# A branch moved between two k-tiles, a split subtraction across it, a weight load on ScalarE's queue and a small chain on GpSimd, in a hybrid decoder layer

## The chip, the core and the metric

One core of a Trainium2 chip runs the whole layer in one launch. The metric is the device time in microseconds (us), the median over runs. The kernel before takes 609.99 us (three runs, 609.93 to 610.08).

## The reference

The inputs are a residual stream x of 512 tokens by 1024, an embedding p of 512 by 256, and the layer's weights, all float32. Cut to what matters here:

```
x = x + hybrid_mixer(rms_norm(x)) @ ...            # GLA heads, gated conv, W_out
h = rms_norm(x); group_logits = h @ w_group + b_group; exp_logits = h @ w_router + b_router
# top 1 of 4 groups, top 2 of the 4 experts in it; weights = p_grp * softmax top 2, renormed
for e in range(16): y += combine[:, e] * ((silu(h @ w_gate[e]) * (h @ w_up[e])) @ w_down[e])
x = x + y
x = x + sigmoid(rms_norm(x) @ w_ple_gate) * (p @ w_ple_proj)   # the embedding product is p @ w_ple_proj
out = rms_norm(x)
```

## The kernel before, in words

Every float32 product is made of three matmuls: operand and weight are each split into a high part (a rounded copy, made by ScalarE) and a low part (value minus high part, a subtraction on VectorE), and TensorE multiplies high by high, high by low and low by high. `Stream` (lines 51 to 150) brings the weights in: `load` (83) takes a free slot and issues a DMA of 1 MB, by default on SyncE's queue (SP); `split` (103) makes the high part at once and returns the low part as a function if `later=True`; the low part of a slot's second half gives the slot back (`give`, 73), and that issues the next load.

The order of work on every engine is the order of the source; nothing is rearranged. Around the change it is this. The mixer's output product ends, its tokens are routed (`route`, `rank`), and meanwhile TensorE computes the embedding product p @ w_ple_proj in sixteen steps `ple(0)` to `ple(15)` (line 810). An output block of 128 x 512 takes two of them, one for each k-tile, of three matmuls each; after the second ScalarE copies the block out of PSUM. The steps fill TensorE's time while VectorE does the routing.

`lo0`, `lo1` and `lo2` (1037, 1048, 1067) are the low parts of the first three half slots of expert 0's gate weights; `lo0` has run early, `lo1` belongs to a second half, so that it gives its slot back, and `lo2` to a first half. `fullest` (948) finds how many tokens the fullest expert has. An expert has 96 places; `overflow` (1174) reads the number into a register on every engine and branches (1177): if an expert has more tokens than that, a handler computes the rest. With these inputs it does not run. The handler calls `weights`, `norms` and `weights2` itself and, in loops, loads 24 pieces of weights by SP (8 for gate, 8 for up, twice 4 for down).

After the branch come the routing weights: `weights` (956; two exponentials on ScalarE among it), `norms` (975; the tokens' RMS factors cut into three bfloat16 parts and put into `vals`, columns 5 to 7), `weights2` (986; columns 2 to 4 of `vals`), a one-hot for expert 2, `lo1`, the last embedding steps, the transposes of expert 0's gathered rows, the matmuls `slots(..., 2, 8)` that read `vals`, `lo2`, and then expert 0's gate product (`pg0`) and 16 experts with it. Two gathers on GpSimd's queue, issued just ahead of the branch, fetch the rows of experts 0 and 1. `W.free.append((ring, "x1")); W.load()` (1269) puts a freed buffer of x to use as a slot, and loads the next weights into it.

Two things of the built program are not seen in the source. Transfers issued by SP and by ScalarE count their completion on eight semaphores in turn, and each transfer waits, on the queue that issues it, until the transfer eight before it has landed. And where a branch is not taken, every engine waits on the way out until its own instructions ahead of the branch are done, and then adds to its semaphores what the handler would have added; SP does this for the eight transfer semaphores, one after the other in a fixed order, and so waits there for every transfer issued ahead of the branch.

Of the kernel before, what the change touches and what calls it, by code (L numbers as in the profile page):

```python
# [14 lines left out]
OP = mybir.AluOpType  # L15
# [3 lines left out]
P = 128  # L19
S = 512  # L20
D = 1024
NT = S // P
# [6 lines left out]
NE = 16  # L29
# [122 lines left out]
def hymba_layer(ctx, tc, x, p, g_mix, w_in, w_gla_gate, b_gla_gate, g_gla_out, w_conv, w_out,  # L152
# [4 lines left out]
    p, w_in, w_out = p[0, 0], w_in[0], w_out[0]  # L157
    ve, se, pe, ge, sy = nc.vector, nc.scalar, nc.tensor, nc.gpsimd, nc.sync
# [15 lines left out]
    def mm_ps(name):  # L174
        return ps.tile([P, HALF], F32, tag="mm", name=name)
# [4 lines left out]
    def half(i):  # L180
        return slice(i * HALF, (i + 1) * HALF)

    def tok(t):
        return slice(t * P, (t + 1) * P)


    W = Stream(nc, hlp, 6)
# [22 lines left out]
    Aa, Af = (consts.tile([P, NT, NG, EPG], BF16, name=f"A{i}") for i in range(2))  # L210
    key = consts.tile([P, NT, NE], F32, name="key")
    iota1 = consts.tile([P, CAP], BF16, name="iota1")
    vals = consts.tile([P, NT, NE, 8], BF16, name="vals")
# [596 lines left out]
    def ple(j):  # L810

        i, k = divmod(j, 2)
        t, ci = divmod(i, 2)
        if j < 2:
            wp.extend(W.take())
        if k == 0:
            pps_[i] = mm_ps(f"pp{t}_{ci}")
        (xh, xl), (wh, wl) = pT[k], wp[k]
        for n, (a, b_) in enumerate(((xh, wh), (xh, wl), (xl, wh))):
            pe.matmul(pps_[i], a[:, tok(t)], b_[:, half(ci)], start=(k + n == 0), stop=(k == 1 and n == 2))  # L820
        if k:
            ple_out(i)
        if j == 15:
            W.done(2)

    def ple_out(i):
        t, ci = divmod(i, 2)
        prj_[t, ci] = prjs[t // 2][1][:, half(2 * (t % 2) + ci)]
        se.copy(prj_[t, ci], pps_[i])
# [100 lines left out]
    def slots(e, oh, vals, toki, rowi, sw, name, c0=0, c1=8, fill=False):  # L930


        pi = aux_ps(f"pslot{name}_{c0}")
        for t in range(NT):
            pe.matmul(pi[:CAP, c0:c1], oh[:, t, :], vals[:, t, e, c0:c1], start=(t == 0), stop=(t == NT - 1))  # L935
        if c0 == 0:
            sv = small.tile([CAP, 1], F32, tag="sv", name="sv" + name)
            ve.tensor_reduce(sv, pi[:CAP, 0:2], axis=AX.X, op=OP.add)
            if fill:
                ve.tensor_scalar(toki[:, e:e + 1], sv, OUT_OF_RANGE, S - 1.0, op0=OP.add, op1=OP.min)  # L940
            ve.tensor_scalar(rowi[:, e:e + 1], sv, OUT_OF_RANGE, None, op0=OP.add)
        if c1 == 8:
            ve.tensor_reduce(sw[:, e], pi[:CAP, 2:8].rearrange("p (w j) -> p w j", j=3), axis=AX.X, op=OP.add)
# [4 lines left out]
    def fullest():  # L948
        cmax = rtp.tile([P, 1], F32, name="cmax", bufs=1)
        ve.tensor_reduce(cmax, pcnt[:, :NE], axis=AX.X, op=OP.max)  # L950
        ve.tensor_copy(cmaxi, cmax)

    wt = []
    sec = rtp.tile([P, NT, NE], BF16, name="sec", bufs=1)
# [19 lines left out]

    def norms():

        r3 = rtp.tile([P, NT, 3], BF16, name="r3", bufs=1)
        left = rtp.tile([P, NT], F32, name="left", bufs=1)
        for j in range(3):
            src = left if j else rsm  # L980
            ve.tensor_copy(r3[:, :, j], src)
            if j < 2:
                ve.tensor_tensor(left, src, r3[:, :, j], op=OP.subtract)
        ve.tensor_copy(vals[:, :, :, 5:8], r3[:, :, None, :].to_broadcast([P, NT, NE, 3]))

    def weights2():
        d_, m, c_, s_ = wt
        z_ = rtp.tile([P, NT], F32, name="z_", bufs=1)
        ve.tensor_reduce(z_, d_, axis=AX.X, op=OP.add)
        ve.scalar_tensor_tensor(z_, m[1], 1.0, z_, op0=OP.add, op1=OP.mult)  # L990
        ve.reciprocal(cw[0], z_)
        ve.tensor_mul(cw[1], cw[0], m[1])

        for d2, a_, c2 in ((c_, Af.rearrange("p t g e -> p t (g e)"), cw[0]), (s_, sec, cw[1])):
            ve.tensor_tensor(d2, a_, c2[:, :, None].to_broadcast([P, NT, NE]), op=OP.mult)
        ve.tensor_tensor(c_, c_, s_, op=OP.add)
        for j in range(2, 5):
            ve.tensor_copy(vals[:, :, :, j], c_)
            if j < 4:
                ve.tensor_tensor(c_, c_, vals[:, :, :, j], op=OP.subtract)  # L1000
# [34 lines left out]
    t = NT - 1  # L1035
# [12 lines left out]
    lo1 = W.split(later=True)  # L1048
# [8 lines left out]
    ple(6)  # L1057
    for e in range(2):
        slots(e, oh01[e], vals, toki, rowi, sw, f"{e}", 0, 2, fill=True)
    ve.tensor_tensor(sec, Aa.rearrange("p t g e -> p t (g e)"), Af.rearrange("p t g e -> p t (g e)"),  # L1060
                     op=OP.subtract)

    pcnt = mm_ps("pcnt")
    for t in range(NT):
        pe.matmul(pcnt[:, :NE], onesb, Aa.rearrange("p t g e -> p t (g e)")[:, t], start=(t == 0), stop=(t == NT - 1))
    fullest()
    lo2 = W.split(later=True)
    mx.close()

# [104 lines left out]
    def overflow(free_x):  # L1174

        many = nc.values_load(cmaxi[0:1, 0:1], min_val=0, max_val=S)
        with tc.If(many > CAP, preferred_fallthrough_block=True, label="crowded"):
            weights()
            norms()
            weights2()  # L1180
            with tc.For_i(0, NE, 1) as ei:
                ke = rt.tile([P, NT], F32, name="ke")
                ve.tensor_copy(ke, key[:, :, bass.ds(ei, 1)].rearrange("p t o -> p (t o)"))
                va_ = rt.tile([P, NT, 8], BF16, name="va_")
                ve.tensor_copy(va_, vals[:, :, bass.ds(ei, 1), :].rearrange("p t o c -> p t (o c)"))

                def product(dst, xT, w, c0, wks):
                    rows_ = w[0, bass.ds(ei, 1)].rearrange("o r c -> (o r) c")
                    for k in range(xT.shape[-1] // CAP):
                        wk = wks[k % len(wks)]  # L1190
                        sy.dma_start(wk, rows_[k * P:(k + 1) * P, c0:c0 + HALF])
                        pe.matmul(dst, xT[:, k * CAP:(k + 1) * CAP], wk, start=(k == 0),
                                  stop=(k == xT.shape[-1] // CAP - 1))

                def turned(dst, src):
                    pt = aux_ps("pt_v")
                    for k in range(4):
                        pe.transpose(pt[:, k * CAP:(k + 1) * CAP], src[:, tok(k)], ident[:CAP, :CAP])
                    ve.tensor_copy(dst, pt[:, :4 * CAP])

                xr, xv, hv, yv = xe[free_x], ye[0][:, :8 * CAP], ye[0][:, :4 * CAP], ye[1][:CAP]
                sv, wa, wb = xr[:CAP, :HALF], xr[:, HALF:], ye[0][:, HALF:]
                with tc.For_i(1, -(-S // CAP), 1):
                    ve.tensor_scalar(ke, ke, float(-CAP), None, op0=OP.add)
                    rw = rt.tile([CAP, 1], I32, name="rw")
                    wv = rt.tile([CAP, 1, 2], F32, name="wv")
                    slots(0, one_hot(0, ke[:, :, None], "v"), va_[:, :, None, :], rw, rw, wv, "v")
                    ge.memset(xr, 0.0)
                    gather(xr[:CAP], rw)
                    for i in range(2):  # L1210
                        turned(xv[:, 4 * CAP * i:4 * CAP * (i + 1)], xr[:CAP, half(i)])
                    pgv, puv = mm_ps("pgv"), mm_ps("puv")
                    product(pgv[:CAP], xv, w_exp_gate, 0, [wa])
                    product(puv[:CAP], xv, w_exp_up, 0, [wa])
                    se.activation(sv, pgv[:CAP], AF.Silu, scale=wv[:, 0, 1:2])
                    ve.scalar_tensor_tensor(sv, puv[:CAP], wv[:, 0, 1:2], sv, op0=OP.mult, op1=OP.mult)
                    turned(hv, sv)
                    for ci in range(2):
                        pdv = mm_ps("pdv")
                        product(pdv[:CAP], hv, w_exp_down, HALF * ci, [wa, wb])  # L1220
                        ve.tensor_scalar(yv[:, half(ci)], pdv[:CAP], wv[:, 0, 0:1], None, op0=OP.mult)
                    scatter(yv, rw)
# [42 lines left out]
    ylast = []  # L1265

    ple(7)
    overflow(0)
    W.free.append((ring, "x1"))
    W.load()  # L1270
    for j in range(8, 11):
        ple(j)
    weights()
    se.preload_act_table_set("silu_and_others")
    norms()
    weights2()
    oh = {2: one_hot(2, key, "2", ve)}
    lo1()
    for j in range(11, 16):
        ple(j)  # L1280
    xTs[0] = transposed(x0[:, half(0)], "xT0a") + transposed(x0[:, half(1)], "xT0b")
    for e in range(2):
        slots(e, oh01[e], vals, toki, rowi, sw, f"{e}", 2, 8)
    lo2()
    W.give((ring, "x0"))
    W.give(pTt[0][0])
    pgs[0] = mm_ps("pg0")
# [34 lines left out]
    e = NE - 1  # L1322
# [181 lines left out]
    t = NT - 1  # L1504
# [63 lines left out]
```

## Time and profile before

| | us |
|---|---|
| median of three runs | 609.99 |
| the profiled execution | 609.77 |
| its span, first to last instruction | 608.1 |

The profiled execution's own time is 1.67 us more than its span, for what lies around it, and 0.22 us under the median. All times of rows are counted from the span's start. In a timeline a row gives start, length, engine, line, operation, what is written and read, and in brackets the idle time ahead of it and what ended it; names with a q (SPq, ACTq) are an engine's queue, which waits, branches and issues DMAs.

### The profile page before, as it was taken

Reading aid. Unit: us, or ns where it says so; the run is one execution under the profiler, and the core shown is the slowest. Engines: PE = TensorE matmul, PEld = TensorE weight load, DVE = VectorE, ACT = ScalarE, POOL = GpSimd, SP = SyncE. Lnnn points to the kernel's source line nnn. Section 1 sums busy time; section 2 is a strip of 40 time slices with the busy share of each in tenths; the row PEclk is TensorE's granted clock in tenths of the full one; section 3 lists DMA queues with packets and bytes.
Section 4 is the critical chain, followed back from the end, with each engine's and each line's share of the span. In section 5 each row is a group of like instructions: output and inputs, shape, how many; then the busy total and the mean of one; then the engine's idle time right before and its main releaser. Section 6 shows DMA issues by size and latency. Waiting matters only on the chain.

```text
span 608.1 us, 8441 instructions
## 1 busy us (share of the span) xinstructions
PE 588.4 (97%) x3026; PEld 450.6 (74%) x3026; DVE 480.1 (79%) x802; ACT 365.0 (60%) x520; POOL 112.6 (19%) x147
## 2 busy tenths in 40 slices
PE   7999999999999999899999999999999999989995
PEld 6997888887687788677777777777777777666884
DVE  4742799874396476799999999999999998879764
ACT  5532537303715333768877888887787897776222
POOL 1440664100420000123210111111011100000111
PEclk9999999999999999999999999999999999999998
DMA  8622221221125948599999999999999989992001
GB/s 282 214 105 71 70 70 69 70 73 68 45 93 210 394 179 306 199 376 361 382 373 364 359 360 345 378 371 360 353 346 357 375 321 373 367 349 85 36 34 70
DMA packets 65292, 146.15 MB, mean 240 GB/s; under 512 B 5205, under 2 KB 5804, under 8 KB 65246
## 3 DMA queue, kind: packets, MB, share of 16 engines
q1 hardware_dynamic: 61342, 136.16, 61.0%
q0 software_dynamic: 3744, 9.15, 6.3%
q8 instruction: 24, 0.39, 0.2%
q10 hardware_dynamic: 160, 0.27, 0.1%
q14 instruction: 22, 0.18, 0.1%
HBM read 137.03 MB, written 12.19 MB: 245 GB/s over the span
## 4 chain that ended last, share of the span: by engine, by line
PE 53%; DVE 4%; issue 1%; ACT 1%; POOLq 0%; DVEq 0%; ACTq 0%
PE pd L1120 15%; PE pg L1120 14%; PE pu L1120 13%; PE pgate L1120 6%; PE pt_xT L1108 2%; PE pgate_last L1521 1%; DVE lo L113 1%; PE pt_hT L1108 1%; DVE lo L118 1%; PE px L1427 1%; ACT hi L112 1%; PE pz L1255 0%; PE pu15b L1344 0%; PE pslot L935 0%; ACT ye L1314 0%
## 5 line engine op out<-in xcount | busy, mean ns | idle before, releaser
L113 DVE TENSOR_TENSOR lo<-raw,hi 128x1024 fp32r<-128x1024 f32 x172 | 203.4, 1218 | 14.1 <-ACT hi L112 14.0
L112 ACT CAST hi<-raw 128x1024 fp32r<-128x1024 f32 x172 | 170.6, 1052 | 0.1
L118 DVE SCALAR_TENSOR_TENSOR lo<-raw,cst,hi 128x512 fp32r<-128x512 f32 (+1 forms) x56 | 44.8, 843 | 16.2 <-ACT hi L117 16.0
L1090 POOL DMA_INDIRECT xe<-xgd,rowi x12 | 19.4, 1614 | 165.0 <-PE pt_xT L1108 158.7
L113 DVE TENSOR_TENSOR lo<-x,hi 128x1024 fp32r<-128x1024 f32 x30 | 36.0, 1219 | 1.7 <-ACT hi L112 1.7
L117 ACT ACTIVATE hi<-raw,cst 128x512 fp32r<-128x512 f32 (+1 forms) x56 | 36.6, 717 | 0.0
L1141 POOL DMA_INDIRECT xd<-ye,rowi x15 | 22.5, 1501 | 49.0 <-ACT ye L1314 45.4
L112 ACT CAST hi<-x 128x1024 fp32r<-128x1024 f32 x30 | 30.8, 1053 | 0.0
L1120 PE MATMUL pg<-hi,xT_1h 128*96 128x512 f32 x60 | 24.4, 407 | 0.0
L1120 PE MATMUL pg<-hi,xT_0h 128*96 128x512 f32 x60 | 23.7, 396 | 0.0
L1120 PE MATMUL pg<-lo,xT_1h 128*96 128x512 f32 x60 | 23.6, 394 | 0.0
L1120 PE MATMUL pg<-hi,xT_1l 128*96 128x512 f32 x60 | 23.6, 393 | 0.0
L1120 PE MATMUL pg<-lo,xT_0h 128*96 128x512 f32 x60 | 23.5, 392 | 0.0
L1120 PE MATMUL pg<-hi,xT_0l 128*96 128x512 f32 x60 | 23.5, 391 | 0.0
L1120 PE MATMUL pu<-hi,xT_0h 128*96 128x512 f32 x56 | 22.9, 409 | 0.0
L1120 PE MATMUL pu<-lo,xT_0h 128*96 128x512 f32 x56 | 22.1, 395 | 0.0
L1120 PE MATMUL pu<-lo,xT_1h 128*96 128x512 f32 x56 | 22.1, 394 | 0.0
L1120 PE MATMUL pu<-hi,xT_1h 128*96 128x512 f32 x56 | 22.1, 394 | 0.0
L1120 PE MATMUL pu<-hi,xT_1l 128*96 128x512 f32 x56 | 22.0, 392 | 0.0
L1120 PE MATMUL pu<-hi,xT_0l 128*96 128x512 f32 x56 | 21.9, 392 | 0.0
L645 ACT ACTIVATE sq<-xs 128x512 f32<-128x512 f32 x4 | 2.5, 631 | 28.5 <-DVE xs L627 28.5
L737 POOL TENSOR_TENSOR xs<-xs,sg 128x128 f32<-128x128 f32 x16 | 11.3, 736 | 44.2 <-ACT sg L732 44.2
(583 smaller groups left out, 1593.7 us busy)
## 6 DMA issues: line engine op xcount, KB each, us to landing
raw<-in_w_exp_gate_dram SPq DMA_DIRECT2D x28, 1024.0 KB, 16.9
raw<-in_w_exp_down_dram SPq DMA_DIRECT2D x27, 1024.0 KB, 13.8
raw<-in_w_exp_up_dram SPq DMA_DIRECT2D x26, 1024.0 KB, 17.8
raw<-in_w_in_dram SPq DMA_DIRECT2D x10, 1024.0 KB, 4.9
x<-in_w_exp_up_dram SPq DMA_DIRECT2D x6, 1024.0 KB, 14.4
x<-in_w_exp_down_dram SPq DMA_DIRECT2D x5, 1024.0 KB, 16.2
xs<-in_x_dram SPq DMA_DIRECT2D x16, 256.0 KB, 5.5
raw<-in_w_out_dram SPq DMA_DIRECT2D x4, 1024.0 KB
```

The costliest lines, as they stand in the source:

```text
L112: self.nc.scalar.copy(hi, rw)
L113: los.append(lambda: eng.tensor_sub(lo, rw, hi.bitcast(F32)))
L117: self.nc.scalar.activation(hi[:, c_], rw[:, c_], AF.Copy, scale=g_)
L118: los.append(lambda c_=c_, g_=g_: eng.scalar_tensor_tensor(lo[:, c_], rw[:, c_], g_, hi[:, c_].bitcast(F32), op0=OP.mult, op1=OP.subtract))
L645: se.activation(osq[c], to[c], AF.Square)
L737: ge.tensor_tensor(tv, tv, sgs[i][:, tok(t)], op=OP.mult)
L1090: ge.indirect_dma_start(out=x_, out_offset=None, in_=xgd, in_offset=bass.IndirectOffsetOnAxis(ap=idx, axis=0), bounds_check=S - 1, oob_is_ ...
L1108: pe.transpose(pt[:, k * n:(k + 1) * n], src[:n, tok(k)], ident[:n, :n])
L1120: pe.matmul(dst, a, b_, start=(k + n == 0), stop=(k == nk - 1 and n == 2))
L1141: ge.indirect_dma_start(out=xd, out_offset=bass.IndirectOffsetOnAxis(ap=idx, axis=0), in_=y_, in_offset=None, bounds_check=S - 1, oob_is_e ...
L1427: pe.transpose(pt[:, tok(k)], X(t)[:, ci * HALF + k * P:ci * HALF + (k + 1) * P], ident)
L1521: pe.matmul(pgl[i][:, :256], a, b_[:, 256 * i:256 * i + 256], start=(k + n == 0), stop=(k == NK - 1 and n == 2))
```

## The change

The branch moves from between `ple(7)` and `ple(8)` to between `ple(8)` and `ple(9)`, the two k-tiles of one block; `lo1` moves ahead of it, `lo2` behind `weights`; `norms` moves to GpSimd and ahead of `weights`; the load into x1's buffer is issued by ScalarE; the subtraction `sec` goes behind `fullest`; in the handler one PSUM block serves both halves of the down product.

```
 def norms():
-            ve.tensor_copy(r3[:, :, j], src)
+            ge.tensor_copy(r3[:, :, j], src)
             if j < 2:
-                ve.tensor_tensor(left, src, r3[:, :, j], op=OP.subtract)
-        ve.tensor_copy(vals[:, :, :, 5:8], ...)
+                ge.tensor_tensor(left, src, r3[:, :, j], op=OP.subtract)
+        ge.tensor_copy(vals[:, :, :, 5:8], ...)
...
-    ve.tensor_tensor(sec, ...)
     pcnt = ...
     fullest()
+    ve.tensor_tensor(sec, ...)
     lo2 = W.split(later=True)
...
+                    pdv = mm_ps("pdv")
                     for ci in range(2):
-                        pdv = mm_ps("pdv")
...
     ple(7)
+    ple(8)
+    lo1()
     overflow(0)
+    ple(9)
     W.free.append((ring, "x1"))
-    W.load()
-    for j in range(8, 11):
-        ple(j)
+    W.load(eng=se)
+    ple(10)
+    norms()
     weights()
     se.preload_act_table_set("silu_and_others")
-    norms()
+    lo2()
     weights2()
     oh = {2: one_hot(2, key, "2", ve)}
-    lo1()
     for j in range(11, 16):
         ple(j)
     ...
-    lo2()
```

## Rows read from the trace of the kernel before

**Rows 1.** The page's busy time of each engine, with its share of the span and its instructions.

```profile
PE 588.4 (97%) x3026; PEld 450.6 (74%) x3026; DVE 480.1 (79%) x802; ACT 365.0 (60%) x520; POOL 112.6 (19%) x147
```

**Rows 2.** The chain of work that ended last, in order of time: start, length, what. The up products of experts 1 and 2 begin here (the second row is cut off by the stretch that was asked for).

```profile
280.53 5.56 PE pu L1120 x24
...
298.41 1.62 PE pu L1120 x7
```

**Rows 3.** Timeline of TensorE: the first embedding matmul behind the branch, the first transpose of expert 0's rows, the slot matmuls, the first and the third matmul of expert 0's gate product.

```profile
248.36 0.47 PE L820 MATMUL pp<-hi,raw 128*128 128x512 f32 x1 [1.49 <-DVEq L1177]
...
254.05 0.49 PE L1108 MATMUL pt_xT0a<-ident,xe 96*128 96x96 f32 x4
...
254.71 0.48 PE L935 MATMUL pslot<-vals,oh 128*96 128x6 bf16 x8
255.26 0.47 PE L1120 MATMUL pg<-hi,xT0ah 128*96 128x512 f32 x1
...
256.24 0.47 PE L1120 MATMUL pg<-hi,xT0al 128*96 128x512 f32 x1 [0.27 <-DVE xT0al L1100]
```

**Rows 4.** The queues at the branch (lines 1176 and 1177): operation, count, shortest, median and longest in ns, first and last start in us.

```profile
L1176 ACTq TENSOR_LOAD <-cmaxi x1: 473/473/473, 246.9 to 246.9; - x1
...
L1177 SPq EVENT_SEMAPHORE  x8: 6/17/703, 248.3 to 249.8; - x8
...
L1177 PEldq COMPARE_BRANCH  x1: 397/397/397, 247.6 to 247.6; - x1
...
L1177 DVEq EVENT_SEMAPHORE  x1: 21/21/21, 248.2 to 248.2; - x1
```

**Rows 5.** Timeline of VectorE ahead of the branch (sec, cmaxi) and behind it: the start of `norms`, the start of `weights2` and its second operation, its last, `lo1`.

```profile
246.47 0.18 DVE L1060 TENSOR_TENSOR sec<-A,A 128x64 bf16<-128x64 bf16 x1
...
246.76 0.15 DVE L951 CAST cmaxi<-cmax 128x1 int32<-128x1 f32 x1
...
249.86 0.17 DVE L981 CAST r<-rsm 128x4 bf16<-128x4 f32 x1
...
251.04 0.16 DVE L989 TENSOR_REDUCE z__2535<-d__2513 128x4 f32<-128x16 f32 x1
251.32 0.16 DVE L990 SCALAR_TENSOR_TENSOR z__2535<-m,z__2535 128x4 f32<-128x4 f32 x1
...
253.77 0.31 DVE L998 CAST vals<-c__2518 128x64 bf16<-128x64 f32 x1
...
254.50 1.22 DVE L113 TENSOR_TENSOR lo<-raw,hi 128x1024 fp32r<-128x1024 f32 x1
```

**Rows 6.** Timeline of ScalarE around the branch: the copy of `ple(7)`'s block, the table load behind the branch, the copy of `ple(9)`'s block, the two exponentials, the next table load.

```profile
246.91 0.58 ACT L829 COPY raw<-pp 128x512 f32<-128x512 f32 x1 [0.57 <-PE pp L820]
247.81 1.28 ACT L829 ACT_TABLE_LOAD   x1 [0.33 <-ACTq L1177]
250.03 0.59 ACT L829 COPY raw<-pp 128x512 f32<-128x512 f32 x1 [0.93 <-PE pp L820]
250.51 0.22 ACT L963 ACTIVATE d__2513<-d__2513 128x16 f32<-128x16 f32 x1
250.63 0.19 ACT L973 ACTIVATE m<-m 128x4 f32<-128x4 f32 x1
250.84 1.28 ACT L1274 ACT_TABLE_LOAD   x1
```

**Rows 7.** SP's queue behind the branch: timeline rows of the load into x1's buffer and of the load into `lo1`'s slot, and, from line 98's own view, the wait ahead of the second (started at 250.4).

```profile
249.95 0.41 SPq L98 DMA_DIRECT2D x<-in_w_exp_up_dram  x1
255.78 0.38 SPq L98 DMA_DIRECT2D raw<-in_w_exp_up_dram  x1
...
L98 SPq EVENT_SEMAPHORE  x1: 5342/5342/5342, 250.4 to 250.4; - x1
```

**Rows 8.** DMA. First what the queue of SP's loads moved in the first and the last of the four microseconds (252 to 253, 255 to 256) in which the load into x1's buffer moved: packets, MB, share of the 16 engines; all four together 500 packets and 1.01 MB. Then the page's issues of two loads of the same size: count, KB each, median us from issue to landing.

```profile
q1 hardware_dynamic: 43, 0.09, 50.6%
...
q1 hardware_dynamic: 124, 0.23, 59.0%
...
raw<-in_w_in_dram SPq DMA_DIRECT2D x10, 1024.0 KB, 4.9
...
raw<-in_w_ple_proj_dram SPq DMA_DIRECT2D x1, 1024.0 KB, 7.9
```

**Rows 9.** A DMA issued by ScalarE's queue (the last output): shortest, median, longest in ns.

```profile
L1540 ACTq DMA_DIRECT2D out_dram<-ye x1: 409/409/409, 604.0 to 604.0; - x1
```

**Rows 10.** The two gathers. GpSimd's timeline row of the second; then, from the view of their tile, us from issue to landing of the first (issued 247.13) and of the second.

```profile
248.57 0.98 POOL L1090 DMA_INDIRECT xe<-xgd,toki  x1 [0.30 <-DVE gm L960]
...
DMA to landing us min/median/max: 4.7/4.7/4.7
...
DMA to landing us min/median/max: 6.5/6.5/6.5
```

**Rows 11.** Elementwise work on GpSimd elsewhere: a one-input operation on 20 columns and a two-input one on 128 columns, shortest, median and longest in ns.

```profile
L323 POOL TENSOR_SCALAR wr<-wr,cst x8: 328/329/385, 30.1 to 32.3; 128x20 f32<-128x20 f32 x8
...
L737 POOL TENSOR_TENSOR xs<-xs,sg x16: 458/904/914, 160.0 to 170.5; 128x128 f32<-128x128 f32 x16
```

**Rows 12.** The end of the span: TensorE's last matmul in its timeline, and one row of the stretches of 1 us, where after the busy times of PE, PEld, DVE, ACT and POOL comes the granted clock of TensorE (1.00 is 2.4 GHz), then the DMA share and GB/s. The rows of the stretches ahead of it have 1.00, those behind it 0.50.

```profile
600.20 0.27 PE L1521 MATMUL pgate_last<-raw,x2l 128*128 128x256 f32 x1
...
603.00:604.00 1.00, 0.00 (x0) 0.00 (x0) 0.72 (x2) 0.72 (x1) 0.25 (x1) 0.55 0.00 0
```

More of the change, by code (lines that the diff above doesn't have):

```diff
@@ L980, in norms @@
             src = left if j else rsm
-            ve.tensor_copy(r3[:, :, j], src)
+            ge.tensor_copy(r3[:, :, j], src)
             if j < 2:
-                ve.tensor_tensor(left, src, r3[:, :, j], op=OP.subtract)
-        ve.tensor_copy(vals[:, :, :, 5:8], r3[:, :, None, :].to_broadcast([P, NT, NE, 3]))
+                ge.tensor_tensor(left, src, r3[:, :, j], op=OP.subtract)
+        ge.tensor_copy(vals[:, :, :, 5:8], r3[:, :, None, :].to_broadcast([P, NT, NE, 3]))
     def weights2():
@@ L1059, in hymba_layer @@
         slots(e, oh01[e], vals, toki, rowi, sw, f"{e}", 0, 2, fill=True)
-    ve.tensor_tensor(sec, Aa.rearrange("p t g e -> p t (g e)"), Af.rearrange("p t g e -> p t (g e)"),
-                     op=OP.subtract)
     pcnt = mm_ps("pcnt")
@@ L1066, in hymba_layer @@
     fullest()
+    ve.tensor_tensor(sec, Aa.rearrange("p t g e -> p t (g e)"), Af.rearrange("p t g e -> p t (g e)"),
+                     op=OP.subtract)
     lo2 = W.split(later=True)
```

## The prediction

> **What bounds the kernel.** I read the page first: TensorE is busy for 97% of the span [rows 1]. Then the chain in order of time: from expert 1 to expert 2 it is TensorE alone, 17.88 us for one expert (298.41 - 280.53), and between 285 and 500 us the waits name none of TensorE's [rows 2]. So what is gained or lost ahead of expert 0 moves everything behind it by as much. Then the timelines between 246 and 256 us, where TensorE does wait: 1.49 us at the branch and 0.27 us ahead of the third matmul of expert 0's gate product [rows 3]. That third matmul, at 256.24, is my mark: the work behind it is the same in both kernels, and I take its shift as the change of the time.
>
> **The parts that help.** `ple(8)` moves into the branch's idle time: three matmuls. Behind the branch TensorE now does 24 in 5.69 us (254.05 - 248.36) [rows 3], 0.237 each, so it saves 0.71 us and reaches the transposes at about 253.35. The branch path itself is some 1.3 us long: the register load starts at 246.9, and VectorE's last wait of it ends at 248.2 [rows 4]. `lo1`, 1.22 us, goes behind `cmaxi` and `sec` on VectorE. It would start at about 246.9 (where `cmaxi` ends now; `sec` behind it gives back at most its own 0.18) and end at 248.1 [rows 5], ahead of VectorE's release at 248.2. That a queue loads its register while its engine works is seen on ScalarE, where both start at 246.9 [rows 4, 6]; if VectorE did not, the branch would come up to 1.2 us later there. Behind the branch VectorE loses `lo1` (1.22) and `norms` (249.86 to 251.04, 1.18) and gets `lo2` (the same shape as `lo1`, 1.22) [rows 5], so it is free for the low part of expert 0's rows 1.18 us sooner.
>
> `norms` on GpSimd: six small operations. No row has these shapes there. The nearest from below is 0.33 us for one input and 20 columns, from above 0.91 us for two inputs and 128 columns [rows 11]; six are 2.0 to 5.5 us, and since the columns are few I take 2.0 and keep 5.5. GpSimd is free when the second gather's issue ends, 249.55 [rows 10], so `vals` has its last columns at 251.5 to 255.0. `weights2` writes the others until 254.08 now [rows 5]. At the lower price this costs nothing, at the upper it is a rival below. The handler's PSUM block costs nothing, since the handler does not run.
>
> **The part that hurts.** `lo1` gives its slot back, and that issues a load of 1 MB on SP: today at 255.78, 0.06 us after `lo1` ends (254.50 + 1.22 = 255.72), SP having stood at that wait for 5.34 us [rows 5, 7]. With `lo1` ahead of the branch, SP issues it at about 248.15, ahead of the branch too. On the way out of the branch SP walks over eight transfer semaphores: that is the x8 row, seven of them over in nanoseconds today since nothing is in flight on them, and the longest 0.70 us [rows 4]. Now one of them belongs to the load just issued, and SP stands there until it has landed.
>
> SP itself could afford that: its next loads were due behind the transposes. But the load into x1's buffer, which the change gives to ScalarE, takes the next semaphore in turn: the load of `lo1`'s slot is the last transfer ahead of the branch, the handler's 24 are three full turns, and x1's is the first behind. Before a transfer is issued its queue waits for that semaphore with the handler's count added, and SP adds this only after it has passed the semaphore ahead of it, the one it stands at. I read this order in the instructions of the program before (there x1's load waits for its semaphore with the handler's count, and SP walks in ascending order), not in a view; the view shows the eight waits, and x1's load directly behind them at 249.95 [rows 4, 7]. So ScalarE, which works in order, stands at its DMA until the other load has landed. Behind it in its queue are the two exponentials, the table load and three copies; VectorE's `weights2` waits for the exponentials, the slot matmuls for `weights2`, and in TensorE's order expert 0's gate product stands behind them.
>
> The Trainium skill says in DMA: Bandwidth & Descriptors, section Anatomy of one DMA, that DMA engines wait on no semaphore and that every such wait is made by the issuing queue ahead of the DMA; the 5.34 us wait on SP's queue agrees [rows 7]. Its section Issuing engines are not separate DMA queues says that a second issuing engine saves only the time of issuing: by that rule the move to ScalarE could be worth at most one issue, 0.41 us [rows 7].
>
> Now the sum for ScalarE's stand. Issue at 248.15. For the landing the nearest row is x1's load today: the same size, the same gathers in flight; issued at 249.95, its last bytes come in the microsecond to 256, so about 5.85 us [rows 7, 8]. The bounds are 4.9 and 7.9 us, other 1 MB loads [rows 8]. I take 5.85: landed at 254.0. Then 0.05 for the semaphores (a guess from rows of 17 ns [rows 4]), ScalarE's issue 0.41 [rows 9]: 254.46. Exponentials 250.51 to 250.82, 0.31 [rows 6]: 254.8. From VectorE's use of the second one to the end of `weights2`, 254.08 - 251.32 = 2.76 [rows 5]: 257.6. Slot matmuls, 255.26 - 254.71 = 0.55 [rows 3]: 258.15. The first two matmuls of the gate product at 0.32 each, as at 248.36 and its successor, 0.64: the third at 258.8. The rows' high part is ready by then on ScalarE (254.8 + table 1.28 + three copies of 0.59 = 257.85, plus 0.5 for the part itself, 258.35) [rows 6], and VectorE's low part shortly behind, inside the same 0.64. So 258.8 - 256.24 = **2.6 us later**; with the bounds, 1.6 and 4.6. The loads lose nothing by it: one is 7.6 us earlier, and x1's at 254.1 still stands ahead of where the second load is now.
>
> The profiled execution took 609.77, 0.22 under the median, so 609.99 + 2.6 = 612.6 is the forecast, and by itself its range is 611.4 to 614.7.
>
> **The rivals.** *The clock falls in the gap.* TensorE would do next to nothing from 254.0 to 257.6, 3.6 us. At the end of the span its last matmul ends at 600.47, and the granted clock falls from 2.4 to 1.2 GHz inside 603 to 604, 2.5 to 3.5 us after it [rows 12]. So the fall can happen here. A matmul of 0.237 would cost as much again; for how many no row shows, and I price it at a stretch as long as the gap itself: 3.6 us at half speed lose 1.8 us, 614.4. The Trainium skill, TensorE: Matmul & The Clock Gate, section What's actually happening, says that the throttled clock is the default and activity releases it; the fall in the tail agrees, and nothing here shows the release. Against it: the gap is little longer than the idle time ahead of that fall.
>
> *Nobody stands.* If x1's load draws a semaphore that SP has passed, or the landing is not waited for, ScalarE issues it at about 249.9 and has the exponentials done by 250.8, as now [rows 6]. `lo2` covers them, `weights2` ends at about 254.0, and TensorE, at the transposes 0.7 us earlier, starts the gate product at about 254.5 and its third matmul, with the low part in time, at 255.15: 1.1 us gained, 608.9, bounds 0.7 and 1.4 (TensorE no longer waits for VectorE's release). That is the other side. For it speaks that the load leaves SP's queue at all; against it the walk over eight semaphores [rows 4]. The price at which it turns is plain: ScalarE's stand costs nothing while the landing comes before 251.4 (254.0 - 2.6), 3.3 us after the issue, and no 1 MB row is under 4.9 [rows 8]. The first gather shares the engines with the earlier load then; its 4.7 us may become the second's 6.5 [rows 10], 253.6 against 253.35, 0.3 us at most.
>
> *GpSimd is the bound.* If nobody stands and `norms` costs 5.5 us, `vals` is full at 255.0, the slots end at 255.6 and the third matmul comes at 256.25: no change, 610.0. If ScalarE stands, 255.0 is before 257.6 and GpSimd is hidden.
>
> **How the numbers follow.** ScalarE stands, clock up: 0.60. It stands and the clock falls: 0.13. Nobody stands: 0.20. GpSimd bounds or the gain is eaten elsewhere: 0.07. A measurement of this kernel can tell about 0.2%, 1.2 us, from no change. The first two are slower by more: 0.73. Of the third, centred on 1.1 us, a little under half is faster by more than 1.2, so 0.09; the rest and the fourth are the same, 0.18. The predicted time is the first case's, 612.6. To hold 8 in 10 the range reaches from the faster case, 608.8, to the first case's upper bound, 614.7, which takes in the fallen clock as well.
>
> **What would show it.** In the changed profile: SP's load of `lo1`'s slot at about 248.2, ahead of SP's walk, and one long wait of 5 to 6 us in that walk; a wait of some 4 us on ScalarE's queue ahead of its DMA, that ends right after SP's; the exponentials at about 254.5, `weights2` ending near 257.6, TensorE idle between the transposes and the slots; `norms` on GpSimd over by 252; `lo1` inside the branch. It is wrong if ScalarE's DMA goes out near 250 and TensorE's third matmul comes before 256.2; then nobody stood. If the walk has its long wait but ScalarE does not, it was the order of the semaphores that I misread. A granted clock under 1.00 behind the gap is the first rival.

## The result, and the profile after

| | us |
|---|---|
| before, median (lowest to highest) | 609.98 (609.93 to 610.08) |
| after, median (lowest to highest) | 616.88 (615.67 to 617.63) |
| ratio, with its 95% interval | 1.0106 [1.0094, 1.0118] |
| the profiled execution of after, and its span | 617.63, 615.9 |

The change costs 6.9 us, 1.1%; the forecast was 612.6. Numbers of lines are one higher than before (1121 for 1120, 1178 for 1177).

**TensorE** first: its timeline, as in [rows 3].

```profile
253.09 0.39 PE L820 MATMUL pp<-hi,raw 128*128 128x512 f32 x1
257.19 0.87 PE L1109 MATMUL pt_xT0a<-ident,xe 96*128 96x96 f32 x4 [3.71 <-DMA xe<-xgd,toki]
...
260.27 0.80 PE L935 MATMUL pslot<-vals,oh 128*96 128x6 bf16 x8 [1.57 <-DVE vals L999]
260.93 0.72 PE L1121 MATMUL pg<-hi,xT0ah 128*96 128x512 f32 x1
...
261.88 0.63 PE L1121 MATMUL pg<-hi,xT0al 128*96 128x512 f32 x1
```

The chain in order of time, expert 1's up product, which answers to the first of [rows 2]:

```profile
288.40 5.56 PE pu L1121 x24
```

TensorE waits twice: 3.71 us for the first gather, ahead of the transposes, then 1.57 us for `vals`, ahead of the slots. The second wait ends last: the gather has landed and is transposed by then. The third matmul of expert 0's gate product, the mark, comes at 261.88, 5.64 us later than in [rows 3]. Expert 1's up product starts 288.40 - 280.53 = 7.87 us later [rows 2], as much as the two executions' own times differ (617.63 - 609.77 = 7.86). So 2.23 us more are lost behind the mark, with no wait named: that is the clock. The stretches of 1 us, columns as in [rows 12], show its fall and its return:

```profile
255.00:256.00 1.00, 0.00 (x0) 0.00 (x0) 0.00 (x0) 0.00 (x0) 0.00 (x0) 1.00 0.80 180
256.00:257.00 1.00, 0.00 (x0) 0.00 (x0) 0.00 (x0) 0.04 (x1) 0.00 (x0) 0.82 0.15 49
257.00:258.00 1.00, 0.81 (x5) 0.84 (x6) 0.62 (x5) 0.98 (x3) 0.00 (x0) 0.50 1.03 45
...
266.00:267.00 1.00, 1.00 (x4) 0.60 (x3) 0.51 (x1) 0.00 (x0) 0.00 (x0) 0.56 1.03 401
267.00:268.00 1.00, 1.00 (x6) 0.73 (x5) 0.00 (x0) 0.00 (x0) 0.00 (x0) 1.00 1.07 424
```

TensorE has been idle since 253.48 (253.09 + 0.39); inside 256 to 257 the granted clock leaves 2.4 GHz for 1.2, and only inside 266 to 267 does it come back. Between, a matmul of the gate product starts every 0.43 us (261.45 to 261.88), where 0.23 is usual.

**SP and ScalarE**, the queues of [rows 4, 6, 7]. First SP's timeline, the load into `lo1`'s slot; then the walk, in the view of its line (columns as in [rows 4]):

```profile
248.41 0.38 SPq L98 DMA_DIRECT2D raw<-in_w_exp_up_dram  x1
```

```profile
L1178 SPq EVENT_SEMAPHORE  x8: 17/17/17, 250.2 to 256.6; - x8
```

And ScalarE's timeline from the copy behind the branch:

```profile
249.42 0.59 ACT L829 COPY raw<-pp 128x512 f32<-128x512 f32 x1
256.49 0.42 ACTq L98 DMA_DIRECT2D x<-in_w_exp_up_dram  x1
256.96 0.22 ACT L963 ACTIVATE d__2523<-d__2523 128x16 f32<-128x16 f32 x1 [6.95 <-SPq L1178]
257.08 0.19 ACT L973 ACTIVATE m<-m 128x4 f32<-128x4 f32 x1
```

The load goes out ahead of the walk; the walk, 1.5 us long before, lasts from 250.2 to 256.6. ScalarE stands behind it: its DMA goes out at 256.49, and the exponentials, at 250.51 before, run at 256.96, after 6.95 us of idle time whose releaser is SP's walk.

**VectorE and GpSimd**, answering to [rows 5, 10, 11]. VectorE's timeline: `lo1`, the first operation behind the branch, the start of `weights2` and its last.

```profile
247.16 1.22 DVE L113 TENSOR_TENSOR lo<-raw,hi 128x1024 fp32r<-128x1024 f32 x1
248.53 0.17 DVE L960 TENSOR_REDUCE gm<-lg 128x4 f32<-128x16 f32 x1
...
257.21 0.17 DVE L990 TENSOR_REDUCE z__2538<-d__2523 128x4 f32<-128x16 f32 x1 [5.84 <-ACT d__2523 L963]
259.91 0.31 DVE L999 CAST vals<-c__2528 128x64 bf16<-128x64 f32 x1
```

GpSimd's timeline: the two gathers, the first and the last operation of `norms`.

```profile
247.46 1.92 POOL L1091 DMA_INDIRECT xe<-xgd,toki  x1 [5.53 <-DVE sec L1066]
249.68 0.98 POOL L1091 DMA_INDIRECT xe<-xgd,toki  x1 [0.30 <-DVE s__2529 L970]
250.67 0.74 POOL L982 CAST r<-rsm 128x4 bf16<-128x4 f32 x1
...
252.57 0.47 POOL L985 COPY vals<-r 128x192 bf16<-128x192 bf16 x1
```

And the first gather's tile: us from issue to landing, 4.7 before.

```profile
DMA to landing us min/median/max: 9.6/9.6/9.6
```

`lo1` lies inside the branch, as forecast. `norms` is over at 253.04, inside the 251.5 to 255.0 of the forecast's sum, though not by 252 as its signs had it. The first gather is not as forecast: issued at 247.46, it lands at about 257.1. What moved in its place stands in the DMA queues (columns as in [rows 8]; q1 carries SP's loads, q0 the gathers), for the microseconds from 250, 251, 252 and 253:

```profile
q1 hardware_dynamic: 134, 0.27, 75.3%
...
q1 hardware_dynamic: 184, 0.38, 98.7%
...
q1 hardware_dynamic: 148, 0.28, 81.7%
q0 software_dynamic: 22, 0.09, 22.0%
...
q0 software_dynamic: 68, 0.25, 90.7%
q1 hardware_dynamic: 28, 0.05, 18.7%
```

In the kernel before, q0 moved 75 packets in 250 to 251; here it moves none until 252.5, when 442 of the load's 528 packets are through, and has most of its packets after 253.

So there are three suspects: ScalarE's stand behind SP's walk, the gather behind the early load, and the clock. The first two run side by side, so one profile can't price them: here the chain that ends last goes through ScalarE's DMA, the exponentials and `vals`, and the gather is hidden behind it, but it might take the chain's place if the stand were gone. My theory is the forecast's, that the stand carries the loss; its rivals are that the gather does, and that the clock does.

### The profile page after: what moved, and what is told of

Read it like the earlier page. It is cut to its first block, busy times and chain, and to the rows that moved or that the text cites. A ratio compares the mean times of both kernels' runs of the same rounds, so it can differ in the third digit from the quotient of the medians.

```text
span 615.9 us, 8438 instructions
## 1 busy us (share of the span) xinstructions
PE 592.7 (96%) x3026; PEld 453.7 (74%) x3026; DVE 479.1 (78%) x796; ACT 365.0 (59%) x520; POOL 115.6 (19%) x153
## 4 chain that ended last, share of the span: by engine, by line
PE 52%; DVE 3%; ACT 1%; issue 1%; POOLq 0%; ACTq 0%; DVEq 0%
PE pg L1121 15%; PE pd L1121 14%; PE pu L1121 13%; PE pgate L1121 5%; PE pt_xT L1109 2%; PE pgate_last L1524 1%; DVE lo L113 1%; PE pt_hT L1109 1%; DVE lo L118 1%; ACT hi L112 1%; PE px L1430 1%; PE pz L1256 0%; PE pslot L935 0%; ACT L1394 0%; ACT ye L1317 0%
## 5 line engine op out<-in xcount | busy, mean ns | idle before, releaser
L118 DVE SCALAR_TENSOR_TENSOR lo<-raw,cst,hi 128x512 fp32r<-128x512 f32 (+1 forms) x52 | 42.1, 849 | 16.2 <-ACT hi L117 16.0
L117 ACT ACTIVATE hi<-raw,cst 128x512 fp32r<-128x512 f32 (+1 forms) x52 | 34.1, 718 | 0.0
L1317 ACT ACTIVATE ye<-pd,sw 96x512 f32<-96x512 f32 x30 | 19.0, 683 | 1.0 <-PE pd L1121 1.0
```

The lines of the kernel that those rows point to most:

```text
L117: self.nc.scalar.activation(hi[:, c_], rw[:, c_], AF.Copy, scale=g_)
L118: los.append(lambda c_=c_, g_=g_: eng.scalar_tensor_tensor(lo[:, c_], rw[:, c_], g_, hi[:, c_].bitcast(F32), op0=OP.mult, op1=OP.subtract))
L1317: se.activation(y_[:, half(ci)], pds[ci][:CAP], AF.Copy, scale=sw[:, e, 0:1])
```

## The experiments

Diffs are against the changed kernel, if nothing else is said. Each time is set against runs of the kernel before on the same chip (medians 610.09 to 610.14); the kernel after itself, run again on one of these chips, took 615.78 (615.54 to 615.91).

**1. The load back on SP.** Takes away ScalarE's stand alone.

```
-    W.load(eng=se)
+    W.load()
```

> The changed kernel, but x1's load is issued by SP again. Theory S (the time is ScalarE's stand at its DMA behind SP's walk): the exponentials run near 250, the slots near 254.5, and the time falls to about 609, under the kernel before. Theory G (the load of lo1's slot, issued just ahead of the branch, also starves the first gather, and TensorE waits for that by itself): the exponentials run near 250 as well, but the transposes still wait for the gather until about 257 and the granted clock still falls; the third matmul of the gate product comes at about 260 instead of 261.9, so some 614.5 to 615.5.

Measured: 614.09 (613.01 to 615.43), ratio 1.0067 [1.0047, 1.0087]. The exponentials run at 249.68. TensorE's timeline at the transposes, and the clock in two stretches:

```profile
256.19 0.87 PE L1109 MATMUL pt_xT0a<-ident,xe 96*128 96x96 f32 x4 [2.93 <-DMA xe<-xgd,toki]
```

```profile
255.00:256.00 1.00, 0.00 (x0) 0.00 (x0) 0.00 (x0) 0.00 (x0) 0.00 (x0) 0.72 0.85 205
256.00:257.00 1.00, 0.81 (x5) 0.84 (x6) 0.00 (x0) 0.00 (x0) 0.00 (x0) 0.50 0.83 94
```

Without the stand the time is 1.7 to 2.8 us shorter (614.09 against 615.78 or 616.88), and 4.0 us of loss stay: the gather alone (8.8 us to landing) keeps TensorE waiting, and the clock falls there too. So what the stand, the whole of my forecast, adds on top is less than the 4.0 us that stay without it.

**2. The slot given back behind the branch.** `lo1` stays ahead of the branch, but its slot is given back, and so the load issued, behind it.

```
-        def rest(n=9):
+        def rest(n=9, give=True):
-            if not los and at is not None:
+            if give and not los and at is not None:
...
-    lo1()
+    lo1(give=False)
     overflow(0)
...
     W.load(eng=se)
+    lo1()
```

> The changed kernel, but lo1's slot is given back only behind the branch: the subtraction itself stays ahead of it, x1's load stays on ScalarE. Theories S and G both have their cause in that load: no long wait in SP's walk, ScalarE's DMA near 250, the first gather landed by 253.4, no fall of the clock, and the gain that was worked out for the other edits, 608.9 (bounds 608.6 to 609.4). Rival: the subtraction beside the gather's issue (1.92 us instead of 1.14), or the load on ScalarE's queue by itself, is what costs: 612 or more.

Measured: 609.22 (608.96 to 612.3), ratio 0.9991 [0.9979, 1.0003]; repeated on another chip, 609.06 (608.85 to 611.64), 0.9992 [0.9981, 1.0004].

> The second experiment once more with more rounds (the changed kernel, lo1's slot given back only behind the branch), to tell its small gain from no change: 609.0 to 609.4, some 0.8 us under the kernel before.

```profile
253.43 0.52 PE L1109 MATMUL pt_xT0a<-ident,xe 96*128 96x96 f32 x4 [0.17 <-DMA xe<-xgd,toki]
...
254.43 0.52 PE L935 MATMUL pslot<-vals,oh 128*96 128x6 bf16 x8 [0.15 <-DVE vals L999]
...
255.40 0.47 PE L1121 MATMUL pg<-hi,xT0al 128*96 128x512 f32 x1
```

In the median the loss is gone with the early load. The mark stands at 255.40, 0.84 us ahead of before; both medians are 0.9 to 1.0 under before, though both intervals just reach 1. SP's load goes out at 249.03, ScalarE's at 249.25, and the gather lands after 6.0 us. The queue of the gathers in 250 to 251, where the load's queue moves nothing:

```profile
q0 software_dynamic: 48, 0.20, 78.3%
```

One of the ten executions and four of the twelve took 611.4 to 612.3. The profile of the second time is of one of these (611.46), and TensorE's timeline there shows the late gather again:

```profile
254.86 0.52 PE L1109 MATMUL pt_xT0a<-ident,xe 96*128 96x96 f32 x4 [1.81 <-DMA xe<-xgd,toki]
```

There the gather's packets also go first, but it lands only after 7.7 us, and the clock falls inside 255 to 256 (0.66). So the load ahead of the branch is not the only way to a late gather; what delayed this one was not tested.

**3. Another turn of the semaphores.** Four transfers of 64 bytes, early on SP, shift the turn by four: the early load now has a semaphore late in SP's walk, and x1's load one that SP has passed by then.

```
+    scr = dram.tile([4, 16], F32, name="scr")
+    for u in range(4):
+        sy.dma_start(scr[u:u + 1, :], brt[0:1, 4:20])
     lo0()
```

> The changed kernel with four transfers of 64 bytes to a scratch in DRAM added behind the writes of x, some 5 us ahead of the branch. They move the load of lo1's slot to the last of the eight semaphores in SP's walk and x1's load to the first. If ScalarE stands because SP adds to x1's semaphore only behind the landing, it now stands until about 250.5 only, and the exponentials run near 251; the first gather stays late, perhaps later for a second load beside it (257 to 259), so 614.5 to 617. If the order of the semaphores does not matter and any transfer ahead of the branch blocks ScalarE, its DMA stays near 256.5 and the time at 616.9.

Measured: 613.59 (612.35 to 614.53), ratio 1.0062 [1.0045, 1.008]. ScalarE's timeline, SP's walk, and TensorE's timeline:

```profile
250.33 0.42 ACTq L98 DMA_DIRECT2D x<-in_w_exp_up_dram  x1
250.81 0.22 ACT L963 ACTIVATE d__2528<-d__2528 128x16 f32<-128x16 f32 x1 [0.84 <-SPq L1181]
```

```profile
L1181 SPq EVENT_SEMAPHORE  x8: 3/17/354, 250.2 to 254.9; - x8
```

```profile
256.05 0.54 PE L1112 MATMUL pt_xT0a<-ident,xe 96*128 96x96 f32 x4 [2.62 <-DMA xe<-xgd,toki]
```

SP still stands in its walk, to 254.9, but ScalarE goes at 250.33, 6.2 us sooner, with every instruction of the change in its place. So the order of the semaphores, which I had read from the program and not from a view, is what made ScalarE stand. The gather stays late, the clock falls (0.50 in 257 to 259), and the time is near that of experiment 1.

**4. The clock held up.** 25 matmuls of `ones` with themselves, whose result nothing uses, fill TensorE's two gaps.

```
+    pw1 = aux_ps("pw1")
+    warm(16, pw1)
     xTs[0] = transposed(x0[:, half(0)], "xT0a") + transposed(x0[:, half(1)], "xT0b")
+    warm(9, pw1)
```

> The changed kernel with 25 small matmuls on constants added in TensorE's gaps, 16 ahead of the transposes and 9 behind them, their result unused. Both gaps stay as long. If the clock's fall is a cost of its own, the granted clock stays at 1.00 and the thirteen gate matmuls that ran at half speed take 0.23 us again: 614.0 to 614.6. If the fall costs nothing, 616.9.

Measured: 614.15 (613.87 to 615.04), ratio 1.007 [1.0054, 1.0087]. The stretches of TensorE's two gaps, in two pieces:

```profile
253.00:257.00 4.00, 4.00 (x38) 3.96 (x37) 1.06 (x7) 1.50 (x3) 0.00 (x0) 1.00 1.02 223
257.00:261.00 4.00, 3.92 (x38) 3.59 (x37) 3.77 (x15) 3.99 (x8) 0.00 (x0) 1.00 0.96 316
```

The clock stays at 2.4 GHz, and the time falls by 1.6 to 2.7 us. The second filling is a little long: `vals` is done at 258.80 and the slots start at 259.42, so about 0.6 of what is left belongs to the filling.

**5. Both: the load on SP and the clock held up** (12 such matmuls ahead of the transposes).

```
-    W.load(eng=se)
+    W.load()
...
+    pw1 = aux_ps("pw1")
+    warm(12, pw1)
     xTs[0] = transposed(x0[:, half(0)], "xT0a") + transposed(x0[:, half(1)], "xT0b")
```

> x1's load on SP as in the first experiment, so that ScalarE does not stand, and 12 small matmuls on constants ahead of the transposes, so that the clock does not fall (their result unused). What is left is the wait for the late first gather: transposes near 256.2, third gate matmul near 258.0 against 256.24, so 611.9 (611.3 to 612.5). If the late gather is not what holds TensorE, it returns to 609.2; if the clock costs nothing, it stays at 614.1.

Measured: 611.98 (610.85 to 612.6), ratio 1.0026 [1.0015, 1.0036]. In the profile, of the shortest execution, the transposes start at 255.64, the clock stays at 1.00, and the mark is here:

```profile
257.32 0.47 PE L1121 MATMUL pg<-hi,xT0al 128*96 128x512 f32 x1
```

Against experiment 1 the clock is worth 2.1 us; against experiment 2, where the early load is gone, the late gather by itself is worth 2.8 us (611.98 - 609.22).

**6. `lo1` back behind the one-hot**, the rest of the change in place.

```
-    lo1()
     overflow(0)
...
     oh = {2: one_hot(2, key, "2", ve)}
+    lo1()
```

> The changed kernel with lo1, subtraction and slot both, back where it was behind the one-hot; ple(8) across the branch, norms on GpSimd, x1's load on ScalarE stay. No load in flight at the branch: ScalarE's DMA near 249.3, no fall of the clock. With the subtraction gone from beside it the first gather's issue takes 1.14 us again instead of 1.92. VectorE's chain is as long as before less norms plus lo2, so the third gate matmul is near 256.2: 609.8 to 610.5. Rival (x1's load on ScalarE's queue or ple(8) across the branch costs): 612 or more.

Measured: 610.14 (609.68 to 611.82), ratio 1.0002 [0.9991, 1.0014]: the loss is gone, and the gain of experiment 2 with it. In the profile the first gather's issue takes 1.14 us again, and it lands after 4.4. GpSimd's timeline, and TensorE's at the mark:

```profile
247.20 1.14 POOL L1091 DMA_INDIRECT xe<-xgd,toki  x1 [5.54 <-DVE sec L1066]
```

```profile
256.30 0.47 PE L1121 MATMUL pg<-hi,xT0al 128*96 128x512 f32 x1 [1.04 <-DVE xT0al L1101]
```

The mark is where it was, now behind VectorE: `lo1` stands ahead of the rows' low part again.

**7. The kernel before, with x1's load on ScalarE alone.**

```
     (against the kernel before)
-    W.load()
+    W.load(eng=se)
```

> The kernel before with one edit: x1's load issued by ScalarE. Nothing is in flight at the branch, so ScalarE waits only until SP's walk ends, some 0.5 us that ScalarE has to spare: 609.8 to 610.4. If a load on ScalarE's queue behind the branch costs by itself, 611 or more.

Measured: 610.11 (609.84 to 611.36), ratio 1.0004 [0.9994, 1.0013]. ScalarE issues at 248.60 and has its exponentials at 250.83, 0.32 us later than before. No cost of a DMA on ScalarE's queue can be measured here, with nothing in flight across the branch.

**8. The kernel before, with `lo1` ahead of the branch alone.**

```
     (against the kernel before)
+    lo1()
     overflow(0)
...
     oh = {2: one_hot(2, key, "2", ve)}
-    lo1()
```

> The kernel before with one edit: lo1, subtraction and slot, ahead of the branch. Its load is in flight at the branch and starves the first gather; x1's load stays on SP and ScalarE does not stand. VectorE is 1.2 us earlier behind the branch, TensorE not. So as in the first experiment: transposes near 256.2, a fall of the clock where the gap is long enough (TensorE has ple(8) still to do, so the gap is 0.7 us shorter): 612.0 to 614.5. If the late gather needs the other edits, 609 to 610.

Measured: 612.54 (611.22 to 612.69), ratio 1.0028 [1.0015, 1.004]. TensorE's timeline, and the clock in three stretches:

```profile
255.90 0.52 PE L1108 MATMUL pt_xT0a<-ident,xe 96*128 96x96 f32 x4 [1.71 <-DMA xe<-xgd,toki]
```

```profile
257.00:258.00 1.00, 1.00 (x5) 0.65 (x4) 1.00 (x4) 1.00 (x2) 0.00 (x0) 0.60 0.75 264
...
259.00:260.00 1.00, 1.00 (x4) 0.61 (x3) 1.00 (x2) 1.00 (x2) 0.00 (x0) 0.50 0.77 268
...
261.00:262.00 1.00, 1.00 (x6) 0.71 (x5) 1.00 (x2) 0.10 (x1) 0.00 (x0) 1.00 0.95 272
```

This one edit brings 2.45 us of loss between the medians (1.7 by the ratio): the gather takes 8.6 us to land, the clock falls, and ScalarE does not stand (exponentials at 250.50).

**9. Experiment 2 with `norms` back on VectorE**, behind `lo2` (its four operations on `ve` for `ge`).

```
     (against experiment 2)
-    norms()
     weights()
     se.preload_act_table_set("silu_and_others")
     lo2()
+    norms()
```

> The second experiment with norms back on VectorE, behind lo2. VectorE's chain to the slots is 1.18 us longer, and the slots wait for vals there already (0.15 us of TensorE's), so 610.1 to 610.5. If GpSimd's chain (2.46 us from 250.45 to 252.90) were in the way itself, the time would be the same or lower: 608.5 to 609.2.

Measured: 610.09 (609.57 to 611.69), ratio 1.0004 [0.9995, 1.0013]. The slots wait for `vals` on VectorE:

```profile
255.13 0.48 PE L935 MATMUL pslot<-vals,oh 128*96 128x6 bf16 x8 [1.09 <-DVE vals L999]
```

So taking `norms` off GpSimd takes back 1.0 us, all that experiment 2 had gained: with `ple(8)` and `lo1` alone TensorE comes to the slots earlier and waits there, 1.09 us, for `vals`.

**10. Experiment 2 with both loads on SP.** x1's buffer is freed but not loaded at once; `lo1`'s second call, behind the transposes in the source, gives its slot back and loads both. Nothing on SP holds these issues there: they go out at 249.01 and 249.51, directly behind the walk.

```
     (against experiment 2)
-    W.load(eng=se)
-    lo1()
...
     xTs[0] = transposed(x0[:, half(0)], "xT0a") + transposed(x0[:, half(1)], "xT0b")
+    lo1()
```

> The second experiment with both loads (x1's and that of lo1's slot) issued by SP behind the transposes, so that the first gather has the DMA engines to itself. The gather lands about 1 us sooner (its issue is still 1.92 us), TensorE's 0.17 us wait for it goes, the 0.15 us for vals stays or takes its place: 608.9 to 609.3, no different from the second experiment within the measurement. If the stream of weights needs those loads early, TensorE waits for weights in experts 1 and 2: 611 or more.

Measured: 609.01 (608.77 to 610.21), ratio 0.9984 [0.9975, 0.9993], 1.1 us under before. It is the one version whose interval lies under 1; from experiment 2 on the same chip (609.06) it can't be told. The number came as expected, the reason given for it did not: the loads were not held back, the gather lands after 6.1 us, no sooner than in experiment 2, and TensorE still waits for it.

```profile
253.42 0.52 PE L1109 MATMUL pt_xT0a<-ident,xe 96*128 96x96 f32 x4 [0.21 <-DMA xe<-xgd,toki]
...
255.35 0.47 PE L1121 MATMUL pg<-hi,xT0al 128*96 128x512 f32 x1
```

The kernel after, run once more beside experiments 5 to 7 (615.78, ratio 1.0087 [1.0071, 1.0104]), had this expectation:

> The changed kernel itself once more, on the same chip as the three below: 615.6 to 617.7.

Its profile (615.90) has the same chain in a shorter form: ScalarE's DMA, TensorE's slots behind `vals`, and the clock in two stretches.

```profile
255.17 0.42 ACTq L98 DMA_DIRECT2D x<-in_w_exp_up_dram  x1
```

```profile
258.96 0.80 PE L935 MATMUL pslot<-vals,oh 128*96 128x6 bf16 x8 [1.77 <-DVE vals L999]
```

```profile
256.00:257.00 1.00, 0.66 (x8) 0.69 (x8) 0.83 (x6) 1.00 (x1) 0.00 (x0) 1.00 0.97 121
257.00:258.00 1.00, 0.19 (x3) 0.00 (x1) 0.86 (x5) 0.99 (x3) 0.00 (x0) 0.85 0.71 268
```

SP issued the load at 248.48 there, the gather landed after 8.7 us, and TensorE waited 2.77 us for it. The mark is at 260.57, and 1.76 us more are lost behind it. The clock was still at 1.00 through 256 to 257 and fell while TensorE waited for `vals`.

## Why the prediction was wrong

The sign and the chain of ScalarE's stand were right; the size was short by 4.3 us in the medians, outside the range. In both profiled executions of the changed kernel the chain that ends last is the one forecast: ScalarE's DMA, the exponentials, `vals`, the slots. Two terms of its sum failed, the landing of the early load, which was mis-sized, and the clock, which the sum had at nothing. The range took in either of the two at its price, not both together.

| us beyond the forecast, by profiled execution | 617.63 | 615.90 |
|---|---|---|
| landing of the early load | 2.15 | 0.77 |
| clock: the last steps to the mark, and behind it | 0.46 + 2.23 | 0.46 + 1.76 |
| later issue of the load | 0.26 | 0.33 |
| small pieces | 0.21 | 0.21 |

A third step failed beside this chain, the first gather: it was priced at 0.3 us at most, and where ScalarE does not stand it costs 2.8.

The experiments, in medians: 609.1 for everything but the early load (experiments 2 and 10), 2.8 for the late gather (5 against 2), 2.1 for the clock (1 against 5), 1.7 to 2.8 for ScalarE's stand on top (after against 1) make 615.7 to 616.8. These are differences of neighbours, so they add up to after whatever the cause, and since the stand and the gather run side by side, another order would give other shares: how long the stand lasts with the gather in time was not run. Experiment 4 gives the last term by another road: its 614.15 less 0.6 of filling is 1.6 over experiment 5.

- **The parts that help: right.** `ple(8)` and `lo1` filled the branch, VectorE came free (248.53 for `gm`, 0.23 later, as all ahead of it was in that execution), `norms` took 1.99 us of GpSimd where 2.0 was taken, though it began 1.1 us later, behind a longer gather issue. The rival "nobody stands" put the whole at 1.1 us, 608.9; experiments 2 and 10, which let nobody stand and no load go early, gave 609.0 to 609.2.
- **SP's walk, the semaphores and ScalarE: right.** Experiment 3 shows the order of the semaphores, 7 and 8 that it takes both edits.
- **The landing: a step that failed, by its size.** "So about 5.85 us", with bounds of 4.9 and 7.9, was 8.0 in one profiled execution (248.41 to 256.4) and 6.6 in the other (248.48 to 255.1); in experiments 4 and 8 it took some 6.8 and 7.0 us to the issue that waited for it. I had taken the row of a load that came behind its gather [rows 8]; this one moved ahead of the gathers, and its last 32 packets beside them, after 253. That this is the reason was not tested.
- **The clock: a step that failed, by being left out of the sum.** The rival's case came true, given 0.13. Its price, 1.8 us, was near: 2.1 in medians, 2.2 and 2.7 in the two profiles. The clock fell in after and in experiments 1, 3 and 8, behind waits of 3.71, 2.93, 2.62 and 1.71 us, so a gap of 3.6 us deserved a higher chance. Whether it would have fallen with the gather in time, behind the transposes, was not run.
- **The gather: a step that failed, hidden here.** "Its 4.7 us may become the second's 6.5 [...], 0.3 us at most." It became 9.6, and TensorE stood 3.71 us. In the changed kernel `vals` comes later still, so this wait is not on the chain that ends last; where ScalarE doesn't stand it decides by itself (experiments 1, 3, 5 and 8). I had let the two transfers share the engines. The rows show an order: most of the load was moved first. So my turning point, a landing before 251.4, was of no use: past it ScalarE is not the only one who is late.
- **The gather's issue was not priced.** It took 1.92 us instead of 1.14 beside `lo1`. Experiments 2, 8, 9 and 10 have `lo1` there and 1.92 too; 6 and 7 have it elsewhere and 1.14. In experiment 2 TensorE waits only 0.17 us for the gather in spite of it. What the early load would do to a gather whose issue is quick was not tried.
- **Two slips without weight.** The bounds 1.6 and 4.6 give 611.6 to 614.6, where the text has 611.4 to 614.7. And the first matmul at 248.36 and its successor lie 0.30 apart, not 0.32.

## What to carry to other kernels

When a change moves the operation that frees a buffer, follow the load that this releases: past which gather it goes out, and across which join of a branch it is still in flight. As an upper bound, price the transfer that comes second by the whole of the first, and not by a share, and then ask which engine has nothing to do until it lands and what its clock does meanwhile. Here the change with the same subtraction at the same place cost 1.1% or, in the median, nothing, by whether its buffer was given back ahead of the branch or behind it. And add rivals that can come true together before a range is drawn.

## What was not expected of the hardware

**Two transfers came one after the other.** In the kernel after the load was issued at 248.41, the gather's issue ended at 249.38 (247.46 + 1.92), and the load's packets went first. In experiment 2 the load was issued at 249.03, the gather's issue ended at 249.16 (247.24 + 1.92), and the gather's went first: 48 packets in 250 to 251, none of the load's. The Trainium skill, DMA: Bandwidth & Descriptors, section Queues, rings and completion order, says that each DMA engine takes turns between the queues for which it has work, packet by packet. The rows from 250 to 252 don't show it, unless the gather's descriptors (the orders for single pieces of the transfer) were not there yet, and no row shows when they were. In the kernel before and in experiment 2 the gather's first packets come 0.5 to 0.8 us after its issue ends; in the kernel after they come only inside 252.5 to 252.75, 3.1 us or more after it.

**VectorE's subtraction lengthened the gather's issue,** 1.92 against 1.14 us. It ran from 247.16 to 248.38, and the issue, begun at 247.46, ended 1.0 us after it. The Trainium skill, SBUF — State Buffer, section SBUF: two separate sides, says that VectorE and GpSimd share one pair of ports, and that a VectorE operation with two inputs in SBUF and a GpSimd one that reads SBUF exclude each other: the first holds the pair to its end, the other is blocked. By that rule the 1.14 would follow the subtraction (inputs `raw` and `hi`; the gather reads `toki`), to 249.52; the trace has 249.38, nearly that.

**The clock came back late and unevenly:** about 10 us after the fall in the profile of 617.63, about 7 in that of 615.90, about 3.5 in experiment 8. In the profile of experiment 6 (611.54, one of its longer executions) it fell, to 0.50 inside 257 to 258, with no wait of TensorE longer than the 1.04 us just ahead of it. The kernel before has such executions too, it seems: beside experiments 8 to 10 five of them took 610.93 to 611.13 us with a mean clock of 0.993, where the shorter ones have 0.995 to 0.998. None of the five was profiled, so what happens in them is open.
